# A routed mixture-of-experts kernel: the first slots' rows partly gathered during the output projection, routing steps reordered, expert numbers by rank read later

## The chip, the cores and the metric

The kernel runs on one core of one Trainium2 chip. The metric is the device time of one execution in microseconds; the time before is the median of three runs, 1043.46 us (1043.24 to 1044.73).

## What is computed

Two residual layers work on 512 tokens of width 1024. Layer 0 mixes the tokens with a gated unit, layer 1 with latent attention; both add a memory attention, and an output projection is added to `x`. Each layer ends with a routed mixture of 32 experts, 2 for each token:

```python
def hierarchical_moe(h, w_group, b_group, w_expert, b_expert, w_gate, w_up, w_down):
    ...
    g_idx = jnp.argmax(g_prob, axis=-1)              # one of 4 groups
    ...
    top_w, top_i = lax.top_k(e_prob, TOP_K)          # 2 of its 8 experts
    top_w = top_w / jnp.sum(top_w, axis=-1, keepdims=True)
    expert_id = g_idx[:, None] * EXPERTS_PER_GROUP + top_i
    weights = g_w * top_w
    combine = jnp.sum(jax.nn.one_hot(expert_id, N_EXPERTS, dtype=jnp.float32) * weights[..., None], axis=1)
    ...
        gate = jnp.einsum('td,edf->tef', xb, w_gate)
        up = jnp.einsum('td,edf->tef', xb, w_up)
        act = jax.nn.silu(gate) * up * cb[..., None].astype(xb.dtype)
        return jnp.einsum('tef,efd->td', act, w_down)
...
    x = x + jnp.concatenate([mix, mem_out], axis=-1) @ w_out
    x = x + hierarchical_moe(rms_norm(x, norm2_g[i]), ...)
```

All is float32. An expert has three weight matrices of 1 MiB, so a layer's experts are about 100 MB.

## The kernel before, in words

The 512 tokens are four row tiles of 128, held in SBUF as `K.x[t]`. TensorE, SP and GpSimd work in the order in which the code is written (`manual`, L1624); VectorE and ScalarE in an order that a scheduler chose. SBUF has 39 shared units for weights; a load into a unit waits until the unit's last reader is done. Stream loads leave from SP's queue.

**Output projection (`w_out`, L570).** Its last three chunks are done tile by tile: for each row tile two halves of three triples of products, then an addition into `K.x[t]` (L609). The function `rows` (L1633) returns steps for slots between the next tile's products: 0 and 1 turn the tile that is just finished for the router (`turn`, L807), 3 makes its logits (L821), 6 chooses its experts (`choose`, L830). `start` (L801) makes a tile's row scale (ScalarE squares, then GpSimd) and stores the tile to `h2d` in DRAM. The last tile has no next one; its steps and all placing are in `finish` (L1642).

**Routing.** `choose` works for batches of tiles ([0, 1], [2], [3]). VectorE finds the two experts and their one-hot marks `osum`; then the weights are made, by VectorE, ScalarE and six GpSimd steps (L883 to L891) that split them into bfloat16 parts in `K.vals`. `begin` (L967) places a batch: products of the marks with a triangle and with ones count the earlier tokens of the same expert (L901), VectorE turns the counts into slot numbers (64 slots for each expert), and builds `of` and `o`, which mark each token's slot. `carry(t)` (L981) multiplies `of` with the tile's rows, so that after four tiles the bank holds the rows of the first 128 slots (experts 0 and 1); it is copied to `x0`, one half by VectorE, the other by ScalarE. `fill` (L995) collects each slot's token number and weights, and `slots` (L1004) reads them.

**Order of experts.** Experts 0 to 5 are loaded before routing is known, during the projection (`ahead`, `rest`, L1659). The other 26 are ordered by how many tokens they have: `rank` (L911) compares their counts on VectorE, TensorE transposes the resulting list (L932), VectorE casts it to `ids` (L944), and SP reads it into registers (`expert`, L954), four or two numbers ahead of each step's loads.

**Expert steps (`moe`, L1036).** There are 14 steps of 128 slots: 3 with two experts by number, 2 with four by rank, 9 with two. A step gathers its rows from `h2d` by an indirect DMA from GpSimd's queue (`gather`, L1043, after a GpSimd memset to zero, since empty slots have an index out of bounds and are skipped), turns them, multiplies with gate and up (`gate_up`, 64 products for two experts), with down, and adds back. Only step 0 takes `x0`. `nxt(i)` lets SP load as many tiles as the steps so far have freed. Loads by number begin at `nxt(1)` in the code, and on SP they stand right behind the last tile's store:

```python
        R = routed(layer, phase, ahead, rest)
        R.g0 = R.slots(R.c0)
        ...
        R.rank()
...
    gather(1)
    xT = turn(0)
    gather(2)
    fills = R.group(1, 0)
    a = gate_up(0, xT)
    fills()
```

Of the kernel before, what the change touches and what calls it, by code (L numbers as in the profile page):

```python
# [13 lines left out]
I32 = mybir.dt.int32  # L14
# [771 lines left out]

class Route:
# [33 lines left out]
    def logits(self, t):  # L821
        K, nc = self.K, self.K.nc
        T = next(T for T in self.BATCHES if t in T)
        if t == T[0]:
            self.b = K.bank([2, 36])
        for k in range(8):
            K.last_mm = nc.tensor.matmul(self.b[:, t - T[0]], self.lg[t][:, k], K.wr[:, k],  # L827
                                         start=k == 0 and t == T[0], stop=k == 7, skip_group_check=True)

    def choose(self, t):  # L830
# [52 lines left out]
        tt(wr[:, :, 1, 0], wr[:, :, 0, 0], ex, ALU.mult, p)  # L883
        p.tensor_copy(wr[:, :, :, 1], bc(self.r[:, T].unsqueeze(2), [n, 2]))

        r1 = z_("r1", [2, 2])
        z = K.vals[:, T]
        p.tensor_copy(z[:, :, :, 2:4], wr)
        tt(r1, wr, z[:, :, :, 2:4], ALU.subtract, p)
        p.tensor_copy(z[:, :, :, 4:6], r1)  # L890
        tt(z[:, :, :, 6:8], r1, z[:, :, :, 4:6], ALU.subtract, p)  # L891
# [19 lines left out]
    def rank(self):  # L911
# [9 lines left out]
        e, w, move = z[:, 5, 0:1], z[:, 5, 2:4], z[:, 6, 0:2 * NT]  # L921
        less = K.k2([n, n], BF, "less")
# [8 lines left out]
        eb = K.bank([n], p=1)  # L931
        K.tr(eb, e[0:n])  # L932
# [10 lines left out]
        self.ids = K.s([n], I32, tag="k_ids", bufs=1, p=1)  # L943
        v.tensor_copy(self.ids, eb)  # L944
# [5 lines left out]
        v.tensor_max(K.over[self.i], w[:, 0:1], w[:, 1:2])  # L950

# [15 lines left out]
    def begin(self, batch):  # L967

        K, T = self.K, self.BATCHES[batch]
        self.place(T)  # L970
        for t in T:
            o, of = K.k1([128], F32, "o1"), K.k1([128], F32, "of")
            sl = self.slot[:, t]
            K.nc.vector.tensor_scalar(o, K.iota16[:, 0:128], sl[:, 0:1], None, op0=ALU.is_equal)
            K.nc.vector.scalar_tensor_tensor(out=of, in0=K.iota16[:, 0:128], scalar=sl[:, 1:2], in1=o, op0=ALU.is_equal,
                                             op1=ALU.add)
            self.of[t] = of
        for t in T:
            self.o[t] = self.mark(0, t)

    def carry(self, t):  # L981

        K = self.K
        if t == 0:
            self.c0 = K.bank([GROUPS[0][1], 8])
            self.b0 = [K.bank([512]) for _ in range(2)]
        for n in range(2):
            K.nc.tensor.matmul(self.b0[n], self.of[t], K.x[t][:, n * 512:n * 512 + 512], start=t == 0, stop=t == NT - 1)
        if t == NT - 1:
            self.x0 = K.k4([D], F32, "xg")  # L990
            K.nc.vector.tensor_copy(self.x0[:, 0:512], self.b0[0])
            K.nc.scalar.copy(self.x0[:, 512:1024], self.b0[1])
# [43 lines left out]
def moe(K, layer, R, X, nxt, on_rows, soon):  # L1036
# [6 lines left out]
    def gather(i):  # L1043
        g, c = place_of(i)
        xg[i] = K.k4([D], F32, "xg")
        K.gate(nc.gpsimd.memset(xg[i], 0.0), K.last_mm)  # L1046
# [84 lines left out]
    xT = turn(0)  # L1131
    gather(2)
    fills = R.group(1, 0)
    a = gate_up(0, xT)
    fills()
# [484 lines left out]
def build(tc, ctx, args, out):  # L1620
# [9 lines left out]
    def routed(layer, phase, ahead=None, rest=None, keep=False):  # L1630
        R = Route(K, layer, keep)

        def rows(t):  # L1633
# [3 lines left out]
            if t == NT - 1 and not keep:  # L1637
                return {0: [finish]}
            return {0: [lambda: R.turn(t, 0)], 1: [lambda: R.turn(t, 1)], 3: [lambda: R.logits(t)],
                    6: [lambda: R.choose(t)]}  # L1640

        def finish():  # L1642
            R.begin(0)
            for q in range(2):
                R.turn(NT - 1, q)
            R.logits(NT - 1)
            R.choose(NT - 1)
            R.carry(0)
            for batch, t in ((1, 1), (2, 2), (None, 3)):
                if batch:  # L1650
                    R.begin(batch)
                R.carry(t)
# [3 lines left out]
    def sparse(layer, phase, on_last, soon=lambda part: None):  # L1656
# [11 lines left out]
        R.rank()  # L1668
# [93 lines left out]
```

## Time and profile before

| | us |
|---|---|
| median of 3 runs | 1043.46 |
| lowest, highest run | 1043.24, 1044.73 |
| the profiled execution | 1043.92 |
| its span, first to last instruction | 1042.1 |
| TensorE busy in the span | 1004.9 |
| VectorE, ScalarE, GpSimd busy | 555.6, 432.6, 195.5 |

The times in the rows count from the start of the span. PE is TensorE, PEld its weight loads, DVE VectorE, ACT ScalarE, POOL GpSimd, SP the engine that issues most DMAs. An idle time in brackets stands before the instruction, with the instruction that ended it. The granted clock is a share of TensorE's full 2.4 GHz. One execution holds both layers, so each place of the change occurs twice: about 250 to 277 us, and about 787 to 813 us.

### The profile page before, as it was taken

How to read it: one execution, taken by the hardware profiler on the slowest of the kernel's cores; microseconds unless marked ns; L12 is line 12 of the kernel's file. 1: busy time of each engine (PE TensorE's matmuls, PEld its weight loads, DVE VectorE, ACT ScalarE, POOL GpSimd, SP SyncE). 2: the span in 40 equal slices, each digit the busy share in tenths (PEclk: the TensorE clock that was granted, in tenths of full speed). 3: DMA queues.
4: the chain of work that ended last, by engine and by line, in shares of the span. 5: the costliest groups of instructions: out<-in, count | busy, mean ns of one | idle time of the engine just before them, and what ended most of it. 6: DMA issues, size and time to landing. Idle time of an engine off the chain costs nothing. (4 is left out here: it accounts for less than half of the span.)

```text
span 1042.1 us, 18418 instructions
## 1 busy us (share of the span) xinstructions
PE 1004.9 (96%) x6438; PEld 743.8 (71%) x6438; DVE 555.6 (53%) x1343; ACT 432.6 (42%) x1172; POOL 195.5 (19%) x415
## 2 busy tenths in 40 slices
PE   8999999999899999999999999999998999999996
PEld 6878888887565666655878888878885666666653
DVE  5654685505464544434767777788027345445343
ACT  6845743414232313213747676778023223223130
POOL 2441110003110101100321553420014001011000
PEclk9999999999999999999999999999999999999998
DMA  9442424694699999999222111204964999999993
GB/s 354 134 139 50 150 71 145 237 409 179 239 408 407 407 407 405 408 407 395 87 54 82 51 28 42 75 18 132 368 278 165 387 408 407 407 407 408 407 404 128
DMA packets 82027, 262.94 MB, mean 252 GB/s; under 512 B 10172, under 2 KB 13472, under 8 KB 81925
## 3 DMA queue, kind: packets, MB, share of 16 engines
q1 hardware_dynamic: 75776, 247.10, 62.2%
q0 software_dynamic: 6144, 14.56, 4.2%
q8 instruction: 53, 0.87, 0.3%
q14 instruction: 50, 0.40, 0.1%
q10 hardware_dynamic: 4, 0.00, 0.0%
HBM read 260.08 MB, written 7.34 MB: 257 GB/s over the span
## 5 line engine op out<-in xcount | busy, mean ns | idle before, releaser
L1073 PE MATMUL ps<-xw,xT 128*64 128x256 f32 (+1 forms) x2048 | 209.6, 382 | 2.8 <-DMA xw<-in_moe_w_up_dram 2.4
L1073 PEld LDWEIGHTS ps<-xw,xT 128*64 128x64 f32 (+1 forms) x2048 | 131.1, 131 | 86.0 <-issue 17.4
L1119 DVE TENSOR_TENSOR x<-x,ps 128x512 f32<-128x512 f32 x216 | 133.4, 680 | 104.7 <-PE ps L1111 104.7
L1097 PE MATMUL ps<-xw,actT 128*64 128x512 f32 (+1 forms) x512 | 102.2, 597 | 0.0
L1110 PE MATMUL ps<-yh,cm 128*128 128x512 f32 x224 | 91.1, 407 | 0.0
L1078 ACT ACTIVATE silu<-ps,wsl 128x256 f32<-128x256 f32 x28 | 13.3, 474 | 183.9 <-PE ps L1073 183.9
L1111 PE MATMUL ps<-yl,cm 128*128 128x512 f32 x224 | 88.1, 393 | 0.1
L1046 POOL MEMSET xg<- 128x1024 f32 x26 | 24.8, 952 | 330.4 <-PE ps L128 278.1
L116 PE MATMUL ps<-wh,c 128*128 128x512 f32 x192 | 76.4, 398 | 0.0
L118 PE MATMUL ps<-wh,c 128*128 128x512 f32 x192 | 74.9, 390 | 0.0
L117 PE MATMUL ps<-wl,c 128*128 128x512 f32 x192 | 74.7, 389 | 0.0
L132 DVE TENSOR_TENSOR yl<-ps,yh 128x512 fp32r<-128x512 f32 x56 | 38.7, 691 | 59.9 <-ACT yh L131 59.9
L1097 PEld LDWEIGHTS ps<-xw,actT 128*64 128x64 f32 (+1 forms) x512 | 29.4, 130 | 52.8 <-issue 39.8
L1059 ACT ACTIVATE xT<-ps,G 128x128 f32<-128x128 f32 x224 | 60.8, 382 | 12.0 <-PE ps L128 11.8
L116 PE MATMUL ps<-wh,hh 128*128 128x512 f32 (+1 forms) x160 | 60.8, 380 | 2.2 <-ACT pm L453 1.1
L219 DVE SCALAR_TENSOR_TENSOR wl<-wr,G,wh 128x512 fp32r<-128x512 f32 (+1 forms) x80 | 55.1, 730 | 11.2 <-ACT wh L209 10.8
L117 PE MATMUL ps<-wl,hh 128*128 128x512 f32 (+1 forms) x160 | 59.8, 374 | 0.0
L118 PE MATMUL ps<-wh,hl 128*128 128x512 f32 (+1 forms) x160 | 59.7, 373 | 0.0
L144 ACT ACTIVATE junk<-x 128x512 bf16<-128x512 f32 x32 | 20.2, 631 | 90.0 <-DVE x L609 87.3
L609 DVE TENSOR_TENSOR x<-x,ps 128x512 f32<-128x512 f32 x16 | 11.0, 687 | 84.6 <-PE ps L118 84.6
L161 POOL TENSOR_SCALAR s1dt.float<-s2dt.float 128x1 f32<-128x1 f32 x18 | 6.9, 381 | 253.1 <-ACT junk L144 252.6
L1110 PEld LDWEIGHTS ps<-yh,cm 128*128 128x128 f32 x224 | 42.1, 188 | 17.0 <-issue 9.3
(369 smaller groups left out, 2046.0 us busy)
## 6 DMA issues: line engine op xcount, KB each, us to landing
xw<-in_moe_w_gate_dram SPq DMA_DIRECT2D x128, 512.0 KB, 10.1
xw<-in_moe_w_up_dram SPq DMA_DIRECT2D x128, 512.0 KB, 10.1
xw<-in_moe_w_down_dram SPq DMA_DIRECT2D x128, 512.0 KB, 10.8
wr<-in_a_w_in_dram SPq DMA_DIRECT2D x20, 512.0 KB, 4.7
wr<-in_a_w_out_dram SPq DMA_DIRECT2D x12, 512.0 KB, 3.4
wr<-in_b_w_out_dram SPq DMA_DIRECT2D x12, 512.0 KB, 3.6
wr<-in_w_mem_kv_dram SPq DMA_DIRECT2D x8, 512.0 KB, 9.9
wr<-in_b_w_in_dram SPq DMA_DIRECT2D x8, 512.0 KB, 10.6
```

The costliest lines, as they stand in the source:

```text
L116: mm(out, A[0], B[0], start=first, stop=False)
L117: mm(out, A[0], B[1], start=False, stop=False)
L118: self.last_mm = mm(out, A[1], B[0], start=False, stop=last)
L132: return self.nc.vector.tensor_sub(lo, src, hi.bitcast(F32))
L219: b = self.nc.vector.scalar_tensor_tensor(out=l, in0=r, scalar=g, in1=h.bitcast(F32), op0=ALU.mult, op1=ALU.subtract)
L1046: K.gate(nc.gpsimd.memset(xg[i], 0.0), K.last_mm)
L1059: nc.scalar.mul(xT[:, k], b[:, k % 4], K.gain(2 + layer, k))
L1073: nc.tensor.matmul(b[c, u], xT[:, k, c], X[i][h][k // 4 * 2 + u][:, k % 4], start=k == 0 and u == 0, stop=k == 7, skip_group_check=True, **tp)
L1097: nc.tensor.matmul(bs[n][c], aT[:, j, c], X[i][h][4 + j][:, n * 512:n * 512 + 512], start=j == 0, stop=j == 1, skip_group_check=True, **tp)
L1110: nc.tensor.matmul(b, cm[:, ts128(t)], yh[:, sl], start=first, stop=False)
L1111: K.last_mm = nc.tensor.matmul(b, cm[:, ts128(t)], yl[:, sl], start=False, stop=last)
L1119: v.tensor_add(K.x[t][:, sl], K.x[t][:, sl], b)
```

## The change

Six things change together. (1) Tiles 0 and 1 are placed (`begin(0)`) during tile 3's projection products, and `early` gathers their rows of the first 128 slots from `h2d` by an indirect DMA into `x0`, which ScalarE has zeroed; `of` and `carry` are left for tiles 2 and 3 alone, whose bank VectorE adds to `x0`. (2) The fills of tiles 0 and 1 follow in `early`. (3) Tile 2's placing stands in the middle of the last tile's logits, tile 3's right after the carry of tile 2. (4) The GpSimd weight steps of tiles 2 and 3 are made later (`R.weights()`), those of tile 2 behind the last tile's row scale. (5) `rank` stands behind `turn(0)`; the transpose of its list and the cast are a new function `numbers`, called after `gate_up(0)`. (6) The zeros of gathers 1 and 2 come from ScalarE.

```diff
+def zeros(K, tile):
+    K.nc.scalar.mul(tile, K.mhalf[:, 0:1].to_broadcast([128, tile.free_size()]), 0.0)
+    return tile
...
-    def logits(self, t):
+    def logits(self, t, mid=None):
...
         for k in range(8):
+            if k == 4 and mid is not None:
+                mid()
...
-    def choose(self, t):
+    def choose(self, t, defer=False):
...
-        tt(wr[:, :, 1, 0], wr[:, :, 0, 0], ex, ALU.mult, p)
-        p.tensor_copy(wr[:, :, :, 1], bc(self.r[:, T].unsqueeze(2), [n, 2]))
...
+        def weights():
+            tt(wr[:, :, 1, 0], wr[:, :, 0, 0], ex, ALU.mult, p)
+            p.tensor_copy(wr[:, :, :, 1], bc(self.r[:, T].unsqueeze(2), [n, 2]))
...
+        self.weights = weights
+        if not defer:
+            weights()
...
         v.scalar_tensor_tensor(out=je, in0=r, scalar=K.col, in1=mine, op0=ALU.is_equal, op1=ALU.mult,
                                accum_out=e)
-        eb = K.bank([n], p=1)
-        K.tr(eb, e[0:n])
...
-        self.ids = K.s([n], I32, tag="k_ids", bufs=1, p=1)
-        v.tensor_copy(self.ids, eb)
...
+    def numbers(self):
+
+        K = self.K
+        eb = K.bank([SORTED], p=1)
+        K.tr(eb, self.e_rank[0:SORTED])
+        self.ids = K.s([SORTED], I32, tag="k_ids", bufs=1, p=1)
+        K.nc.vector.tensor_copy(self.ids, eb)
...
         self.place(T)
-        for t in T:
+        for t in T if batch else ():
             o, of = K.k1([128], F32, "o1"), K.k1([128], F32, "of")
...
+    def early(self):
+
+        K, nc = self.K, self.K.nc
+        v = nc.vector
+        self.x0 = zeros(K, K.k4([D], F32, "xg"))
+        b = K.bank([8])
+        for t in self.BATCHES[0]:
+            for j in range(2):
+                nc.tensor.matmul(b, self.o[t][:, j, 0:128], K.vals[:, t, j], start=(t, j) == (0, 0),
+                                 stop=(t, j) == (1, 1))
+        tok, idx = K.s([1]), K.s([1], I32, tag="idx0", bufs=1)
+        v.tensor_reduce(tok, b[:, 0:2], axis=AX.X, op=ALU.add)
+        v.tensor_scalar(idx, tok, 1024.0, 0.0, op0=ALU.add, op1=ALU.max)
+        nc.gpsimd.indirect_dma_start(
+            out=self.x0, out_offset=None, in_=K.h2d[self.i][0:256],
+            in_offset=bass.IndirectOffsetOnAxis(ap=idx, axis=0), bounds_check=255, oob_is_err=False)
+        self.c0 = K.bank([GROUPS[0][1], 8])
+        for t in self.BATCHES[0]:
+            self.fill(self.c0, t, self.o[t])
+
     def carry(self, t):
...
-            self.x0 = K.k4([D], F32, "xg")
-            K.nc.vector.tensor_copy(self.x0[:, 0:512], self.b0[0])
-            K.nc.scalar.copy(self.x0[:, 512:1024], self.b0[1])
+            for n in range(2):
+                x0 = self.x0[:, n * 512:n * 512 + 512]
+                K.nc.vector.tensor_add(x0, x0, self.b0[n])
...
-        K.gate(nc.gpsimd.memset(xg[i], 0.0), K.last_mm)
+        if i < 3:
+            zeros(K, xg[i])
+        else:
+            K.gate(nc.gpsimd.memset(xg[i], 0.0), K.last_mm)
...
     xT = turn(0)
+    R.rank()
     gather(2)
     fills = R.group(1, 0)
     a = gate_up(0, xT)
+    R.numbers()
     fills()
...
             if t == NT - 1 and not keep:
+                R.weights()
                 return {0: [finish]}
...
+            todo = {0: [lambda: R.turn(t, 0)], 1: [lambda: R.turn(t, 1)], 3: [lambda: R.logits(t)],
+                    6: [lambda: R.choose(t, t == 2 and not keep)]}
+            if t == 2 and not keep:
+                todo[2] = [lambda: R.begin(0)]
+                todo[6].insert(0, R.early)
+            return todo
 
         def finish():
-            R.begin(0)
             for q in range(2):
                 R.turn(NT - 1, q)
-            R.logits(NT - 1)
-            R.choose(NT - 1)
-            R.carry(0)
-            for batch, t in ((1, 1), (2, 2), (None, 3)):
-                if batch:
-                    R.begin(batch)
-                R.carry(t)
+            R.logits(NT - 1, lambda: R.begin(1))
+            R.choose(NT - 1, True)
+            R.carry(2)
+            R.begin(2)
+            R.weights()
+            R.carry(3)
...
         nc.scalar.activation(K.s([1]), R.ex[:, 0:1], AF.Silu)
-        R.rank()
```

## Rows read from the trace of the kernel before

**Rows 1.** The page of the profile: the first line of its part 1, then one line of its part 2 (busy tenths of the DMA engines in 40 equal slices of the span), and one line of part 6 (the loads of gate tiles: count, KB each, median us from issue to landing).

```profile
PE 1004.9 (96%) x6438; PEld 743.8 (71%) x6438; DVE 555.6 (53%) x1343; ACT 432.6 (42%) x1172; POOL 195.5 (19%) x415
...
DMA  9442424694699999999222111204964999999993
...
xw<-in_moe_w_gate_dram SPq DMA_DIRECT2D x128, 512.0 KB, 10.1
```

**Rows 2.** Busy time of the engines in two stretches of the first expert stage. Columns: stretch and its length, busy us (instructions) of PE, PEld, DVE, ACT and POOL, granted TensorE clock, DMA share, GB/s.

```profile
275.00:300.00 25.00, 24.96 (x196) 15.02 (x194) 11.19 (x27) 8.37 (x24) 1.95 (x2) 1.00 1.03 408
...
450.00:475.00 25.00, 24.65 (x158) 16.00 (x156) 12.30 (x21) 6.75 (x21) 2.46 (x4) 1.00 1.02 406
```

**Rows 3.** DMA queues in 300 to 470 us: the line of the indirect gathers' queue (packets, MB, share of 16 engines).

```profile
q0 software_dynamic: 1584, 3.35, 5.2%
```

**Rows 4.** Timeline of the SP queue (start, us, line, operation, tile, count): the first and the last expert loads by number of layer 0, and the first of layer 1.

```profile
270.79 2.62 SPq L254 DMA_DIRECT2D xw<-in_moe_w_gate_dram  x4
...
471.95 4.19 SPq L254 DMA_DIRECT2D xw<-in_moe_w_down_dram  x4
...
807.07 2.68 SPq L254 DMA_DIRECT2D xw<-in_moe_w_gate_dram  x4
```

**Rows 5.** The chain of work that ended last, in the second expert stage (start, us, what): the first and the last of its three stretches of DMA, and what follows the last.

```profile
875.98 11.16 DMA xw<-in_moe_w_up_dram
...
989.41 11.27 DMA xw<-in_moe_w_up_dram
1000.73 3.24 PE ps L1073 x26
```

**Rows 6.** What SP waited for in 268 to 500 us (us in total, times, longest).

```profile
SPq L954 <- DVE rank L936: 16.5, 1, 16.5
SPq L254 <- PE ps L1073: 7.9, 15, 2.4
```

**Rows 7.** Timeline of VectorE in layer 0, from the last tile's choice of experts to the cast of the expert numbers.

```profile
256.17 0.26 DVE L843 SCALAR_TENSOR_TENSOR c_L<-ps,rr,br 128x36 f32<-128x36 f32 x1 [1.39 <-POOL rr L152]
...
259.16 0.30 DVE L963 TENSOR_SCALAR os<-iota,rs 128x384 bf16<-128x384 f16 x1
...
260.68 1.13 DVE L963 TENSOR_SCALAR os<-iota,rs 128x384 bf16<-128x384 f16 x1
...
263.29 0.69 DVE L991 COPY xg<-ps 128x512 f32<-128x512 f32 x1 [0.99 <-PE ps L988]
...
264.48 0.17 DVE L1013 TENSOR_SCALAR idx<-tok 128x3 int32<-128x3 f32 x1
...
267.83 0.17 DVE L944 CAST k_ids<-ps 1x26 int32<-1x26 f32 x1
```

**Rows 8.** The register loads of line 954 on SP over the whole run (ns min/median/max, first and last start in us).

```profile
L954 SPq TENSOR_LOAD <-k_ids x52: 261/267/468, 268.0 to 995.5; - x52
```

**Rows 9.** Timeline of TensorE in layer 0, from the last row tile's transposes to the second step's products (start, us, line, operation, tile, count, idle time before it and its releaser), and one line of layer 1.

```profile
250.53 1.60 PE L128 MATMUL ps<-ident,x 128*128 128x128 f32 x8
251.97 2.24 PE L827 MATMUL ps<-wr,hT 128*128 128x36 f32 x16
...
259.60 0.18 PE L901 MATMUL ps<-os,tri 128*128 128x32 bf16 x1 [1.35 <-DVE os L839]
...
262.12 1.98 PE L988 MATMUL ps<-x,of 128*128 128x512 f32 x4 [0.40 <-DVE of L975]
...
266.95 0.18 PE L128 MATMUL ps<-ident,rank 26*1 26x26 f32 x1 [2.60 <-DVE rank L929]
267.06 1.74 PE L128 MATMUL ps<-ident,xg 128*128 128x128 f32 x8
268.74 8.19 PE L1073 MATMUL ps<-xw,xT 128*64 128x256 f32 x64
...
278.52 5.40 PE L1073 MATMUL ps<-xw,xT 128*64 128x256 f32 x48
...
284.29 1.95 PE L1073 MATMUL ps<-xw,xT 128*64 128x256 f32 x16
...
805.52 7.75 PE L1073 MATMUL ps<-xw,xT 128*64 128x256 f32 x64
```

**Rows 10.** Timeline of GpSimd in layer 0, from the weights of tile 2 to the first gather.

```profile
253.29 0.38 POOL L839 TENSOR_TENSOR rw<-rw,c_ex 128x1 f32<-128x1 f32 x1 [1.36 <-DVE rw L882]
...
254.92 0.29 POOL L161 TENSOR_SCALAR s1dt.float<-s2dt.float 128x1 f32<-128x1 f32 x1
...
255.57 0.57 POOL L152 TENSOR_TENSOR rr<-s1dt.float,mhalf 128x1 f32<-128x1 f32 x1
...
260.76 0.95 POOL L1046 MEMSET xg<- 128x1024 f32 x1
265.50 1.18 POOL L1047 DMA_INDIRECT xg<-h2d,idx  x1 [3.79 <-DVE wsl L1015]
```

**Rows 11.** All indirect gathers of layer 0 in 225 to 500 us: time from issue to landing.

```profile
DMA to landing us min/median/max: 4.0/7.6/8.2
```

**Rows 12.** The columns of group 2 again, for three stretches around the first expert product of layer 0.

```profile
254.00:256.00 2.00, 2.00 (x13) 0.95 (x13) 0.78 (x4) 0.00 (x0) 1.61 (x7) 1.00 1.03 422
268.00:270.00 2.00, 2.00 (x10) 1.18 (x10) 1.97 (x12) 2.00 (x8) 0.96 (x1) 0.50 0.54 150
272.00:274.00 2.00, 2.00 (x22) 1.31 (x20) 0.00 (x0) 0.00 (x0) 0.00 (x0) 1.00 0.88 246
```

More of the change, by code (lines that the diff above doesn't have):

```diff
@@ L882, in choose @@
         v.reciprocal(wr[:, :, 0, 0], den)
-        tt(wr[:, :, 1, 0], wr[:, :, 0, 0], ex, ALU.mult, p)
-        p.tensor_copy(wr[:, :, :, 1], bc(self.r[:, T].unsqueeze(2), [n, 2]))
[L886 to L891, printed above, removed]
+        def weights():
+            tt(wr[:, :, 1, 0], wr[:, :, 0, 0], ex, ALU.mult, p)
+            p.tensor_copy(wr[:, :, :, 1], bc(self.r[:, T].unsqueeze(2), [n, 2]))
+            r1 = z_("r1", [2, 2])
+            z = K.vals[:, T]
+            p.tensor_copy(z[:, :, :, 2:4], wr)
+            tt(r1, wr, z[:, :, :, 2:4], ALU.subtract, p)
+            p.tensor_copy(z[:, :, :, 4:6], r1)
+            tt(z[:, :, :, 6:8], r1, z[:, :, :, 4:6], ALU.subtract, p)
+        self.weights = weights
+        if not defer:
+            weights()
     def place(self, T):
@@ L921, in rank @@
         e, w, move = z[:, 5, 0:1], z[:, 5, 2:4], z[:, 6, 0:2 * NT]
+        self.e_rank = e
         less = K.k2([n, n], BF, "less")
@@ L979, in begin @@
             self.o[t] = self.mark(0, t)
+    def early(self):
[16 more added lines that the diff above has]
+            self.fill(self.c0, t, self.o[t])
     def carry(self, t):
         K = self.K
-        if t == 0:
-            self.c0 = K.bank([GROUPS[0][1], 8])
+        if t == 2:
             self.b0 = [K.bank([512]) for _ in range(2)]
         for n in range(2):
-            K.nc.tensor.matmul(self.b0[n], self.of[t], K.x[t][:, n * 512:n * 512 + 512], start=t == 0, stop=t == NT - 1)
+            K.nc.tensor.matmul(self.b0[n], self.of[t], K.x[t][:, n * 512:n * 512 + 512], start=t == 2, stop=t == NT - 1)
         if t == NT - 1:
-            self.x0 = K.k4([D], F32, "xg")
-            K.nc.vector.tensor_copy(self.x0[:, 0:512], self.b0[0])
-            K.nc.scalar.copy(self.x0[:, 512:1024], self.b0[1])
+            for n in range(2):
+                x0 = self.x0[:, n * 512:n * 512 + 512]
+                K.nc.vector.tensor_add(x0, x0, self.b0[n])
         self.fill(self.c0, t, self.o[t])
@@ L1637, in rows @@
             if t == NT - 1 and not keep:
+                R.weights()
                 return {0: [finish]}
-            return {0: [lambda: R.turn(t, 0)], 1: [lambda: R.turn(t, 1)], 3: [lambda: R.logits(t)],
-                    6: [lambda: R.choose(t)]}
+            todo = {0: [lambda: R.turn(t, 0)], 1: [lambda: R.turn(t, 1)], 3: [lambda: R.logits(t)],
[4 more added lines that the diff above has]
+            return todo
         def finish():
-            R.begin(0)
             for q in range(2):
                 R.turn(NT - 1, q)
-            R.logits(NT - 1)
-            R.choose(NT - 1)
-            R.carry(0)
-            for batch, t in ((1, 1), (2, 2), (None, 3)):
-                if batch:
-                    R.begin(batch)
-                R.carry(t)
+            R.logits(NT - 1, lambda: R.begin(1))
[4 more added lines that the diff above has]
+            R.carry(3)
         phase(K, rows, ahead)
```

## The prediction

> **What bounds the kernel now.** I read the page first: TensorE is busy 96% of the span, but the DMA line shows two long runs of nines, one for each expert stage [rows 1]. The windows of the first stage decide between the two. TensorE is busy nearly all the time, and the DMA engines have a share of 1.02 to 1.03 at 406 to 408 GB/s from 275 us to 475 us [rows 2]. So the DMA has no free time there. The bytes agree: 26 experts are loaded by number, 6 tiles of 512 KB (0.524 MB) each [rows 1], 81.8 MB; eleven gathers of about 0.335 MB (3.35 MB for ten [rows 3]) add 3.7 MB; 85.5 MB at 407 GB/s are 210 us. The first of these loads leaves SP at 270.79, the last ends at 476.1 [rows 4] and lands about 10 us later [rows 1]: 215 us with start and landing. The chain says the same of layer 1: its pieces on the expert weights end at 887.1 and at 1000.7, and only TensorE's tail follows [rows 5]. The expert stage is thus a stream whose end is its start plus its bytes, and TensorE keeps its pace.
>
> What starts the stream? SP waited 16.5 us for one thing, the expert numbers by rank [rows 6]. The numbers' cast runs from 267.83 to 268.00 [rows 7], the register loads begin at 268.0 [rows 8], and the first load follows at 270.79, 2.8 us after the cast.
>
> **The change, first half: TensorE's start.** Before, the stretch from the last projection product to the first expert product at 268.74 is a chain through all engines. Times are of layer 0; layer 1 repeats it.
>
> Row scale of the last tile. The logits are done at 254.2 [rows 9], but VectorE's first step on them starts at 256.17, after 1.39 us for the row scale [rows 7]: GpSimd did six weight steps of tile 2 from 253.29, and the scale only from 254.92 to 256.14 [rows 10]. The change puts the weights behind the scale, but the early gather and two small subtractions ahead of it. The gather's index needs four small products and two VectorE steps after the last projection product: about 251.7 (an estimate). Before, a gather started 0.85 us after its index (264.65 to 265.50) and took 1.18 [rows 7, 10]. So the early one runs from 252.5 to 253.7, the subtractions to 254.2, the scale (1.22) to 255.4. Gain 0.7; bounds 0 and 2.0 (logits at once).
>
> Choice of the last tile, 256.17 to the placing product at 259.60: 3.43 us. VectorE's placing of tile 2 lies among these steps (one marking alone is 0.30 [rows 7]); it moves ahead, since its product now stands inside the logits. Gain 0.6; bounds 0 and 1.1. Placing to the carry product, 259.60 to 262.12: 2.52 us, with one marking at 1.13 instead of 0.30 while GpSimd's memset runs from 260.76 [rows 7, 10]. ScalarE now writes those zeros; gain 0.8; bounds 0 and 0.8.
>
> The removed carries of tiles 0 and 1, two times 1.98 us of TensorE, are worth nothing: they lay where it later waited 1.35 us at 259.60 [rows 9]. The marks and first fills go under the projection, whose products run on. The carry product (1.98) now starts at 260.0 instead of 262.12 and ends at 262.0; the second of the two additions (0.69, as the copy at 263.29) ends at 262.7. The gathered rows must be there at 261.1. Gathers took 4.0 to 8.2 us [rows 11], and the last prefetched expert is still loading then, DMA share 1.03 [rows 12]; issued at 252.5 they land by 256.5 to 260.7, just in time.
>
> Ranking leaves the path. TensorE waited 2.60 us for it ahead of the first gathered rows [rows 9]. The first half of these can now turn while the second is added; from the second addition I take 0.9 us to the first expert product (1.68 before from turn to product; bounds 0.65 and 1.7). So the product starts at 263.6 instead of 268.74: **5.1 us earlier**, in layer 1 at 800.4 instead of 805.52. The 4 small counting products of the ranking now precede it and fit while ScalarE scales the turned rows.
>
> **The change, second half: the stream's start.** The numbers are now transposed after all 64 products of the first step. Those took 8.1 us in layer 0 and 7.7 in layer 1 [rows 9]. Transpose and cast (0.18 and 0.17 [rows 9, 7]) with hand-overs are 0.5, then SP's 2.8. First load: 263.6 + 8.1 + 0.5 + 2.8 = 275.0 against 270.79, **4.2 us later**; layer 1: 800.4 + 7.7 + 0.5 + 2.8 = 811.4 against 807.07, 4.3 later. Something is regained: before, the ramp was slow (246 GB/s in 272 to 274 [rows 12]) because the fourth and later loads waited for tiles still being read; now eight tiles are free at once. I take 0.7 per layer, between 0 and 1.0. Delay of the stream: 3.5 + 3.6 = **7.1 us**. What waits behind SP's register load is every later load, and behind these the products of the fourth step on; TensorE's lead of 5.1 us ends in waits for weights. The ScalarE zeros (about 1 us each, an estimate from the memset's 0.95 [rows 10]) lie in its idle time; if they did not, the second and third gather would be late by that much, and these are needed a step later.
>
> One thing can shift this. The clock was 0.50 in 268 to 270 [rows 12], the lower level (1.2 GHz), after TensorE had waited; the first step took 8.19 us, the second step's two pieces only 5.40 + 1.95 = 7.35 [rows 9]. I keep the slow figure since the waits that precede it remain. The Trainium skill ("TensorE: Matmul & The Clock Gate", "What's actually happening") calls the throttled clock the default, released by activity; by that the removed carries make the start colder, not warmer, and the trace's 0.50 after a wait agrees. At the full clock the delay would be 0.4 to 0.8 us less per layer.
>
> **Sum.** The profiled execution took 1043.92 us, its span 1042.1. 1043.92 + 7.1 = 1051.0; the median of the three runs is 0.46 lower, so 1050.6. All good bounds at once (product 7.2 us earlier, full clock, ramp 1.0) still delay the stream by 0.4 and 0.9: 1044.8. All bad ones (gather late, gains lost, product only 2.2 earlier, the cast 1 us behind another VectorE step, no ramp gain) give 8.1 + 8.2: 1059.8. Half way on either side is 1047.7 to 1055.2.
>
> **Rivals.** *TensorE is the bound.* Then its lead stays: 1043.5 - 2 x 5.1 = 1033.3. For it: 96% busy, and SP waited 7.9 us on products [rows 6], so tiles, not bytes, may hold the stream. Against: the share of 1.03 while it did so. It decides if DMA share falls below 1 in mid stage. The Trainium skill ("Perfetto Trace Analysis", "Identifying the Most-Contended Engine") holds matmul busy time for no measure of closeness to the bound; no run so far shows that here by itself. Chance 0.12.
>
> *The later stream catches up.* An earlier TensorE frees tiles sooner, so SP's 7.9 us of waits on products vanish; if half of each layer's were bytes lost, that repays 3.5 us per layer: 1043.5. Against it again the saturated share. Chance 0.07.
>
> *The early rows do not come early.* If the gather lands after about 263.5 (behind the last expert's tiles, or behind the store of tile 2), the first product starts hardly earlier and the numbers still come after it: about 1060. Chance 0.05.
>
> The forecast has 0.76. A change under 0.2% (2.1 us) is no change for this measurement. Faster is the first rival, 0.12; same the second, 0.07; slower the rest, 0.81. The range 1043.5 to 1055.5 holds nearly all of the forecast and the second rival.
>
> **What the changed profile would show.** The first expert product near 263.6 and 800.4; the numbers' transpose behind its 64 products; the first load by number near 275.0 and 811.4; the hole in DMA before it longer; the share in the stage still 1.03; TensorE's waits for expert weights up by about 8.6 us per layer (5.1 + 3.5), in the fourth to sixth step; the chain passing through these loads. The forecast is wrong if the first load leaves no later than before, or if it does and the stage ends no later.

## The result, and the profile after

The changed kernel takes 1055.76 us, the median of five runs (1053.49 to 1058.18), against 1044.57 (1043.24 to 1044.86) for the kernel before on the same chip: a ratio of 1.0112, with a 95% interval of 1.0098 to 1.0125. It is slower, as forecast, but by 11.2 us and not by 7.1, and 0.3 us outside the range. The profiled execution of the changed kernel took 1053.49 us, span 1051.8; it is the fastest of the five, so the trace below explains 9.6 us against the traced execution of before, and what the slower ones add is read from the run a_again.

The page after, with its lines for TensorE and for the DMA engines (40 slices), against [rows 1]:

```profile
PE 1007.6 (96%) x6430; PEld 741.8 (71%) x6430; DVE 555.4 (53%) x1341; ACT 437.3 (42%) x1176; POOL 194.5 (18%) x413
...
DMA  9432423794699999999222111213954999999993
```

TensorE's 96% is unchanged although the kernel is 9.7 us longer in span. The share of a whole run again says nothing. The Trainium skill ("Perfetto Trace Analysis", "Identifying the Most-Contended Engine") calls matmul busy time no good measure of how close a kernel is to the roofline, and here the trace agrees: 96% before, 96% after.

The windows after, columns as in [rows 2]: two early stretches that answer to [rows 12], the two of [rows 2], and one in between.

```profile
254.00:256.00 2.00, 0.77 (x1) 0.50 (x2) 1.90 (x14) 0.00 (x0) 0.52 (x3) 0.75 1.02 408
256.00:258.00 2.00, 2.00 (x4) 0.73 (x3) 0.83 (x6) 0.20 (x1) 0.94 (x5) 0.50 0.72 283
...
275.00:300.00 25.00, 25.00 (x189) 14.67 (x185) 9.90 (x23) 5.74 (x15) 1.96 (x2) 1.00 1.00 382
325.00:350.00 25.00, 20.24 (x204) 10.34 (x196) 9.20 (x21) 4.59 (x13) 1.96 (x2) 1.00 1.03 406
450.00:475.00 25.00, 23.77 (x157) 14.88 (x154) 8.87 (x16) 4.67 (x13) 2.47 (x4) 1.00 1.03 408
```

Two things are to be seen. Once the stream runs, the DMA engines are as full as before (1.03, 406 to 408 GB/s), and now TensorE has holes: 4.8 us of 25 in 325 to 350, where it was busy for all 25.00 before. And ahead of the expert stage the granted clock falls to 0.50, the 1.2 GHz level, in 256 to 258, after a stretch in which TensorE was busy 0.77 of 2 us; before, it was busy for all of 254 to 256 [rows 12].

The SP queue after (the loads of [rows 4]: first of layer 0, last of layer 0, first of layer 1), then SP's wait for the numbers and its longest wait on products in 268 to 500 us, against [rows 6]:

```profile
274.34 2.23 SPq L254 DMA_DIRECT2D xw<-in_moe_w_gate_dram  x4
...
476.00 4.20 SPq L254 DMA_DIRECT2D xw<-in_moe_w_down_dram  x4
...
816.67 2.24 SPq L254 DMA_DIRECT2D xw<-in_moe_w_gate_dram  x4
```

```profile
SPq L972 <- DVE k_ids L968: 21.3, 1, 21.3
SPq L254 <- PE ps L1113: 5.1, 17, 0.4
```

The first load by number is 3.55 us later than before, the last 4.05, the first of layer 1 9.60. SP's wait for the numbers is 21.3 us where it was 16.5.

TensorE after, against [rows 9]:

```profile
255.23 3.55 PE L1025 MATMUL ps<-x,of 128*128 128x512 f32 x4 [1.89 <-DVE of L993]
...
258.84 0.18 PE L914 MATMUL ps<-os,tri 128*128 128x32 bf16 x1
260.56 1.98 PE L1025 MATMUL ps<-x,of 128*128 128x512 f32 x4 [1.54 <-DVE of L993]
...
262.54 1.54 PE L128 MATMUL ps<-ident,xg 128*128 128x128 f32 x8
...
264.10 7.13 PE L1113 MATMUL ps<-xw,xT 128*64 128x256 f32 x64
271.16 0.18 PE L128 MATMUL ps<-ident,rank 26*1 26x26 f32 x1
...
806.70 7.13 PE L1113 MATMUL ps<-xw,xT 128*64 128x256 f32 x64
```

The last projection product starts at 248.58 in this execution and at 250.21 in that of before, a difference between executions and not of the change: in a_again, the same changed kernel, it starts at 250.32. So I measure each layer from its own last projection product, P (layer 1: 790.77 after, 786.75 before).

| us after P, layer 0 / layer 1 | before | after |
|---|---|---|
| first expert product | 18.53 / 18.77 | 15.52 / 15.93 |
| first load by number | 20.58 / 20.32 | 25.76 / 25.90 |
| end of the last load's issue | 225.93 / 225.54 | 231.62 / 231.18 |
| last row less the row above it | 205.35 / 205.22 | 205.86 / 205.28 |

This closes the sum. The stream starts 5.18 us later in layer 0 and 5.58 in layer 1, and takes 0.51 and 0.06 longer: 11.33. Less the 1.63 us by which this execution reached P earlier, that is 9.70, the difference of the spans. TensorE's head start of 3.0 and 2.8 us appears nowhere in it.

The chain that ended last, in layer 1, against [rows 5]: it still passes through the expert weights, the last such piece ends at 1010.3, and TensorE's tail follows.

```profile
885.59 10.78 DMA xw<-in_moe_w_up_dram
...
999.55 10.78 DMA xw<-in_moe_w_up_dram
1010.38 3.24 PE ps L1113 x26
```

### The profile page after: what moved, and what is told of

Its sections match the earlier page's. It is cut to its first block, busy times and chain, and to the rows that moved or that the text cites. A ratio compares the mean times of both kernels' runs of the same rounds, so it can differ in the third digit from the quotient of the medians.

```text
span 1051.8 us, 18406 instructions
## 1 busy us (share of the span) xinstructions
PE 1007.6 (96%) x6430; PEld 741.8 (71%) x6430; DVE 555.4 (53%) x1341; ACT 437.3 (42%) x1176; POOL 194.5 (18%) x413
## 3 DMA queue, kind: packets, MB, share of 16 engines
q0 software_dynamic: 6432, 14.83, 4.2%
## 5 line engine op out<-in xcount | busy, mean ns | idle before, releaser
L1113 PE MATMUL ps<-xw,xT 128*64 128x256 f32 (+1 forms) x2048 | 215.3, 383 | 12.4 <-DMA xw<-in_moe_w_up_dram 11.5
L1086 POOL MEMSET xg<- 128x1024 f32 x22 | 20.9, 952 | 340.7 <-PE ps L128 297.0
```

The lines of the kernel that those rows point to most:

```text
L1113: nc.tensor.matmul(b[c, u], xT[:, k, c], X[i][h][k // 4 * 2 + u][:, k % 4], start=k == 0 and u == 0, stop=k == 7, skip_group_check=True, **tp)
```

## The experiments

Each starts from the changed kernel or from the kernel before, as its edit says. First the table of what they measured, all offsets from P (layer 0 / layer 1), since every verdict below rests on it.

| run | us, median (range) | ratio to before, 95% | first product | first load by number | load to last load |
|---|---|---|---|---|---|
| a_mid | 1050.89 (1049.38–1052.34) | 1.0061 [1.0044, 1.0078] | 17.56 / 15.41 | 25.62 / 23.21 | 205.1 / 204.9 |
| b_late | 1052.82 (1051.21–1053.86) | 1.0078 [1.0061, 1.0095] | 15.28 / 15.28 | 25.52 / 25.25 | 205.1 / 205.6 |
| b_static | 1041.45 (1037.37–1044.38) | 0.9972 [0.9958, 0.9987] | 18.80 / 18.79 | 1.58 / 1.56 | |
| a_static | 1035.26 (1034.29–1037.16) | 0.9919 [0.9902, 0.9935] | 17.55 / 15.28 | 1.80 / 1.78 | |
| a_warm | 1052.63 (1051.74–1054.49) | 1.0100 [1.0080, 1.0121] | 15.43 / 15.24 | 25.67 / 25.22 | 205.4 / 205.5 |
| a_warm_choice | 1053.73 (1051.68–1055.15) | 1.0098 [1.0076, 1.0121] | 15.37 / 15.09 | 25.61 / 25.07 | 205.0 / 205.6 |
| a_rank_warm | 1041.98 (1039.11–1043.87) | 0.9986 [0.9974, 0.9997] | 19.02 / 16.48 | 20.89 / 18.08 | 206.3 / 206.5 |
| b_rank | 1041.01 (1039.72–1043.63) | 0.9984 [0.9973, 0.9995] | 16.28 / 16.28 | 18.15 / 17.89 | 205.6 / 207.2 |
| a_again | 1056.07 (1054.40–1057.42) | 1.0111 [1.0092, 1.0130] | 17.55 / 17.04 | 27.79 / 27.01 | 205.3 / 205.0 |
| a_choice2 | 1051.44 (1051.10–1052.63) | 1.0072 [1.0051, 1.0093] | 14.51 / 14.23 | 24.75 / 24.20 | 204.8 / 205.7 |
| a_best | 1045.04 (1041.89–1048.05) | 1.0013 [1.0000, 1.0027] | 15.05 / 14.78 | 20.55 / 20.00 | 205.7 / 206.2 |
| b_best | 1045.94 (1044.35–1047.23) | 1.0011 [1.0001, 1.0021] | 15.27 / 15.27 | 21.89 / 21.57 | 205.2 / 205.0 |

The kernel before took 1044.45 beside the first four, 1043.37 beside the next four and 1043.78 beside the last four.

The last column is the theory in one place. With the numbers known only at run time, first products from 14.2 to 19.0 us after P and first loads from 17.9 to 27.8 gave streams of 204.8 to 207.2 us. The streams of 206.2 us and more all have a first load at 20.9 us or sooner, so a part of an early start is given back.

**a_mid: the numbers half a step earlier.**

```diff
-    a = gate_up(0, xT)
-    R.numbers()
+    a = gate_up(0, xT, {4: R.numbers})
```

> The kernel after, with the numbers' transpose and cast in the middle of the first step's products (ahead of the 5th of 8 chunks) instead of behind them. Theory A (the stream of expert loads starts 2.8 us after the numbers' cast, and the stage ends with the stream): the cast comes 3.5 us earlier in each layer (half of 7.1 us of products), the first load by number near 270.9 us on the changed kernel's time scale, the run 6.9 us shorter: about 1048.9. Theory B (the 11 us come from TensorE's waits and its lower clock after them, or from work that the change added, not from the stream's start): no change, about 1055.8.

Measured 1050.89. In layer 1 the first load came 2.7 us earlier after P than in the changed kernel's trace (half of the first step's products take 3.6), and the last load 3.1 us earlier (228.10 against 231.18). In layer 0 it came hardly earlier, because in this execution both carries ran at the low clock and the first product was 2 us late. The sign is the theory's; its size has two further causes. One is the carries, which the next pairs take apart. The other is the cast: the transpose ran at 270.52 in layer 0 and at 810.67 in layer 1, the cast only at 272.03 and 812.18, 1.5 us later, since VectorE still had markings ahead of it. In the changed kernel it is 0.2 us later (271.16 to 271.37). That is 1.3 of the 3.6 us.

**b_late: of the whole change, the late numbers alone.** The kernel before, with only the transpose and the cast of the numbers taken out of the ranking and put behind the first step's products.

```diff
-        eb = K.bank([n], p=1)
-        K.tr(eb, e[0:n])
...
+    def numbers(self):
...
     a = gate_up(0, xT)
+    R.numbers()
```

> The kernel before, with one part of the change alone: the numbers' transpose and cast behind the first step's products. Theory A: TensorE does not wait 2.6 us for the ranking, so the first product starts near 266.4 instead of 268.74, its 64 products end near 274.5, the first load follows near 277.8 instead of 270.79; 7.0 us later in each layer: about 1058.6. Theory B: the first product is 2.3 us earlier and nothing else is worse: 1040 to 1044.

Measured 1052.82, 8.4 us over before, so this part alone makes most of the loss. TensorE in layer 0 of it:

```profile
262.78 1.33 PE L128 MATMUL ps<-ident,xg 128*128 128x128 f32 x8
264.05 7.13 PE L1078 MATMUL ps<-xw,xT 128*64 128x256 f32 x64
271.10 0.18 PE L128 MATMUL ps<-ident,rank 26*1 26x26 f32 x1
```

The first product came 15.28 us after P in both layers, 3.3 to 3.5 us earlier than before and as early as the changed kernel's, with no early gather, no deferred weights and all four carries still there. So what TensorE gains in the changed kernel is the ranking's 2.60 us off its path [rows 9], and the rest of the first half brought it nothing in sum; its parts, below, cancel. I had expected this kernel slower, since I gave the product a smaller lead and its products 8.1 us; they took 7.1.

**b_static and a_static: no numbers to wait for.** The kernel before and the changed kernel with the experts taken in a fixed order, so the weights used are not those that the routing asks for. The work and the bytes are the same.

```diff
-                ids = [R.expert(rank + h) for h in range(WIDTH[i])]
+                ids = [FIXED + rank + h for h in range(WIDTH[i])]
```

> The kernel before, but the loads by number take experts 6 to 31 in fixed order, so SP waits for no numbers; the sorting has then no effect on which weights are used. Same bytes, same products. Theory A: the stream is now started by free tiles: three spare tiles load early, the rest as the first step frees them, an effective start some 2.5 to 3 us earlier per layer: 1038 to 1040, unless TensorE's own pace takes over (then 1040 to 1042). Theory B: SP's wait was not what counted: 1044.6.

> The kernel after with the same fixed order of experts, so that the place of the numbers does not count. Theory A: all of the 11 us go, and the first product, about 3 us earlier per layer than before, frees tiles that much earlier: 4 to 6 us below the kernel before with fixed order, 1033 to 1036. Theory B: still 8 to 11 us above the kernel before with fixed order.

Measured 1041.45 and 1035.26. Waiting for the numbers cost the kernel before 3.0 us and the changed kernel 20.5 (against its 1055.76). Two readings follow. In the kernel before, the free tiles held the stream nearly as late as the numbers did: without the numbers its last load ends 0.7 and 1.4 us earlier after P (225.22 and 224.18 against 225.93 and 225.54), and no more. And with the numbers out of the way, an earlier first product does free tiles earlier: a_static takes 6.2 us less than b_static. One window shows where, first of b_static and then of a_static, columns as before:

```profile
260.00:285.00 25.00, 21.95 (x171) 13.69 (x171) 10.26 (x37) 5.43 (x19) 4.11 (x5) 0.86 0.58 211
```

```profile
260.00:285.00 25.00, 24.84 (x193) 14.67 (x193) 10.47 (x39) 7.18 (x21) 2.17 (x2) 0.92 0.70 261
```

The stream fills earlier, 261 against 211 GB/s around the first product (262 where the window is moved by the 1.55 us by which a_static reaches P sooner). In both runs three loads leave for tiles that are free, the early ones of the table; the fourth waits for a tile that the first step frees, and leaves 24.22 and 22.67 us after P in b_static, 20.82 and 18.55 in a_static. So the early start would have been worth 6 us, had the stream not been tied to the numbers.

**a_again: the changed kernel once more.** Nothing edited.

> The changed kernel once more, unaltered, beside the next three. Theory C (TensorE idles before the carry of tile 2 and its clock falls): that carry takes 3.5 to 3.8 us instead of 1.98 in both layers; the carry of tile 3 takes 1.98 or 3.8 as it falls, and with 3.8 the first product comes 17.5 instead of 15.5 us after the last projection product. Median 1053.5 to 1056, runs spread over 4 us.

Measured 1056.07, the same as the first five runs' 1055.76 within their spread; the profiled execution took 1056.98. Its carries in layer 0, and one window:

```profile
256.95 3.78 PE L1025 MATMUL ps<-x,of 128*128 128x512 f32 x4 [1.88 <-DVE of L993]
...
262.54 3.78 PE L1025 MATMUL ps<-x,of 128*128 128x512 f32 x4 [1.54 <-DVE of L993]
```

```profile
262.00:264.00 2.00, 1.46 (x2) 0.84 (x3) 0.71 (x3) 0.00 (x0) 0.00 (x0) 0.50 0.00 0
```

Here the second carry too ran at clock 0.50 and took 3.78 us instead of 1.98, so the first product came 17.55 us after P instead of 15.52 and the first load 27.79 instead of 25.76: 2.0 us, which is the difference of the carries plus 0.2. Of the changed kernel's five first runs the slowest (1058.18) has the lowest mean clock, 0.981, and the fastest 0.991. The lead of the change thus varies from execution to execution with the clock, and the median of 1055.76 lies between this execution and the one first traced.

**a_warm: TensorE kept busy.** The changed kernel with four products of no use, three ahead of tile 2's carry and one ahead of tile 3's.

```diff
+        def warm(n):
+            b = K.bank([512])
+            for _ in range(n):
+                nc.tensor.matmul(b, K.ident, K.x[0][:, 0:512], start=True, stop=True)
...
+            warm(3)
             R.carry(2)
             R.begin(2)
+            warm(1)
```

> The kernel after, with four spare products (ident times a row tile, read by nobody) put where TensorE waits: three ahead of the carry of tile 2, one ahead of the carry of tile 3. Theory A with C (the removed carries had kept TensorE at the full clock; without them it idles, falls to 0.50, and the carries of tiles 2 and 3 take up to 3.8 us instead of 1.98, differently from run to run): both carries take 1.98 in both layers, the first product comes 15.3 to 15.5 us after the last projection product in both layers, the first load by number 25.3 to 25.6 after it, runs within 2 us of each other, median 1053 to 1054. Rival (the spread of the runs has another cause): 1055.8 and a spread of 4 to 5 us as before.

The carries of layer 0:

```profile
255.59 1.88 PE L1025 MATMUL ps<-x,of 128*128 128x512 f32 x4
...
260.24 1.98 PE L1025 MATMUL ps<-x,of 128*128 128x512 f32 x4 [0.58 <-DVE of L993]
```

Both carries are at 1.9 to 2.0 us in both layers, and the first product is at 15.43 and 15.24. Over all traces with the carries of tiles 0 and 1 gone: without spare products (the changed kernel, a_again, a_mid, a_static) tile 2's carry is slow, at 3.5 us or more, in all eight stages; with them (a_warm, a_warm_choice, a_choice2, a_best, a_rank_warm) both carries are at 1.9 to 2.0 in nine of ten. So the slow carries are those at the low clock, and products in TensorE's wait mostly prevent it. That this makes the kernel faster is not shown: 1052.63 is 3 us under the changed kernel's median, but the intervals of the two ratios overlap.

**a_warm_choice and a_choice2: the last tile's choice.** In the changed kernel VectorE waited for one subtraction of GpSimd. Here it does that subtraction itself, and tile 3 is placed ahead of tile 2's carry; three spare products stand ahead of the placing. a_warm_choice has the fourth one too, ahead of tile 3's carry; a_choice2, whose edit this is, leaves it out.

```diff
-        tt(g, Lg, bc(gm.unsqueeze(2), [n, 4]), ALU.subtract, p)
+        tt(g, Lg, bc(gm.unsqueeze(2), [n, 4]), ALU.subtract)
...
+            warm(3)
+            R.begin(2)
             R.carry(2)
-            R.begin(2)
```

> The same, and two more steps: the subtraction ahead of the group softmax runs on VectorE instead of GpSimd (where it stands behind the six weight steps of tile 2), and tile 3 is placed before the carry of tile 2. If the lost part of TensorE's lead is that wait and that order: placing of tile 3 1.1 to 1.5 us earlier, first product 14.0 to 14.5 us after the last projection product, first load 24.2 to 24.7 after it, about 2 us less than with the spare products alone: 1051 to 1052. Otherwise no change against it.

> The kernel after with three spare products ahead of tile 3's placing, that placing ahead of tile 2's carry, and the subtraction before the group softmax on VectorE. Nothing stands ahead of the carry of tile 3 but tile 2's. If VectorE's 1.08 us wait for that softmax is what ate the rest of TensorE's lead: first product 14.3 to 14.6 us after the last projection product, first load 24.5 to 24.8 after it, 0.7 to 1 us less per layer than with spare products alone (1052.6): about 1051. If not, 15.3 and 25.5 again.

a_warm_choice missed its expectation. The placing product moved from 10.19 to 9.02 us after P, but tile 2's carry and the spare product now stood between it and tile 3's carry on TensorE's queue, and the first product stayed at 15.37. Without the spare one (a_choice2) it came at 14.51 and 14.23, about 1 us earlier, the first load at 24.75 and 24.20, and the time was 1051.44. VectorE's wait is gone in it, and the last tile's choice takes 3.75 us (255.59 to 259.34 in layer 0) where it takes 4.94 in the changed kernel. The gain of about 1 us per layer is that of the three steps together, the subtraction, the order and the spare product left out; their shares in it are not separated.

**b_rank and a_rank_warm: the numbers early.** The ranking ahead of the last carry, and its transpose and cast at once behind that carry, in the kernel before (b_rank) and in a_warm (a_rank_warm).

```diff
+                    R.rank()
                 R.carry(t)
...
+            R.numbers()
...
-        R.rank()
```

> The kernel before with the early ranking alone: counting products and ranking ahead of the carry of tile 3, the numbers' transpose right behind it. Theory A: numbers' cast near 15.5, first load near 18.5, first product near 17 us after the last projection product: 1040 to 1042, about as good as the changed kernel with the same ranking, so the early gather and the reordering bring nothing that the ranking's place does not. Rival (they do bring TensorE a lead): 2 us or more slower than that kernel.

> The kernel after with the spare products, and the ranking started as soon as tile 3's experts are known (ahead of its carry), the numbers' transpose behind that carry and ahead of the first turn. Theory A: the numbers are cast some 16 us after the last projection product, the first load leaves about 19 us after it (before 20.4, after 25.8); TensorE's first product waits for the transpose and comes at about 17. The stream is then held by free tiles, about 2 us per layer earlier than before: 1040 to 1041, faster than both kernels. Theory B: no better than after with spare products.

TensorE in layer 0 of b_rank:

```profile
264.44 0.18 PE L128 MATMUL ps<-ident,rank 26*1 26x26 f32 x1 [0.94 <-DVE rank L933]
264.55 1.23 PE L128 MATMUL ps<-ident,xg 128*128 128x128 f32 x8
265.75 0.44 PE L1078 MATMUL ps<-xw,xT 128*64 128x256 f32 x2
```

The wait for the ranking shrank from 2.60 us to 0.94, and both the product and the load came 2.2 to 2.5 us earlier than before. The kernel took 1041.01, a ratio of 0.9984 [0.9973, 0.9995]: faster than both kernels, but only by 2.4 us (1.7 by the ratio) where the load moved 2.4 us in each of two layers. In layer 0 the last load ended 2.2 us earlier (223.71 after P). In layer 1 only 0.4, its stream being the longest of all, 207.2 us, and its ramp is where that lies:

```profile
800.00:825.00 25.00, 24.96 (x215) 16.43 (x215) 10.76 (x40) 9.37 (x30) 3.25 (x3) 1.00 0.88 330
```

The window begins 2.80 us ahead of the first load. The same stretch of before (804.27 to 829.27) had 352 GB/s; 22 GB/s less for 25 us are 0.55 MB, or 1.4 us of stream. In layer 0 it is 340 against 350 GB/s. Longer waits for free tiles do not show in this ramp: from the first load on, SP waited 2.6 us in 25 for TensorE's work, against 7.3 before, and 9.7 for earlier loads, against 6.6. What slowed the ramp, and why it cost layer 1 more than layer 0, is open.

a_rank_warm came to 1041.98, the same as b_rank. It is 13.8 us under the changed kernel and 10.7 under a_warm, from which it differs only in the place of the ranking and of the numbers. That is the cleanest verdict: this place makes the loss. With the ranking early, the early gather and the reordering bring nothing more.

**a_best and b_best: early ranking, transpose behind the first products.**

```diff
-    a = gate_up(0, xT)
-    R.numbers()
+    a = gate_up(0, xT, {1: R.numbers})
...
+            R.rank()
             R.carry(3)
```

> As the run with the subtraction on VectorE, and with the ranking begun ahead of tile 3's carry and the numbers' transpose behind the first of the 8 chunks of the first step's products, so that neither waits for the other. Theory A: first product 15.0 to 15.5, first load 19.0 to 19.8 us after the last projection product; the stream is then held by free tiles alone, as with experts in fixed order (1035.3): 1036 to 1039, below both kernels. Theory B: no better than 1042.

> The kernel before with the early ranking and the numbers' transpose behind the first chunk of the first step's products, nothing else of the change. Theory A: first product 15.3 to 15.8, first load 19.2 to 20 us after the last projection product: 1037 to 1040, within 2 us of the kernel with all other parts of the change. If the early gather and the reordering do count, 2 us or more slower than that.

Both missed: 1045.04 and 1045.94. In layer 1 of a_best TensorE turned the numbers at 801.90; VectorE's part shows why it didn't help:

```profile
802.40 1.09 DVE L981 TENSOR_SCALAR os<-iota,rs 128x512 bf16<-128x512 f16 x3
803.41 0.17 DVE L968 CAST k_ids<-ps 1x26 int32<-1x26 f32 x1
```

The cast ran 1.5 us after the transpose, behind four slot markings that had been scheduled ahead of it. In layer 0 of b_best it was 2.7 us (265.68 to 268.33). The product's lead over b_rank, 1.0 to 1.5 us, bought nothing; the load's delay of 2.1 to 3.7 us per layer cost 3 us in the whole by the ratios to before (4 to 5 by the medians). This is the change's own exchange, on a smaller scale. Against the kernel before, a_best shows it with the loads held still: they leave at 20.55 and 20.00 us after P, before at 20.58 and 20.32, the first products come 3.5 and 4.0 us earlier, and the time is the same (1.0013 [1.0000, 1.0027]).

## Why the prediction was right about the mechanism and wrong about the size

**The bound.** Right. The stream by number lasts 205 to 207 us from its first load, with first products from 14.2 to 19.0, and the time follows the first load. *TensorE is the bound* is refuted by b_late and a_rank_warm, whose first products are as early as or later than the changed kernel's while the times follow the loads, and by a_best, whose early products gain nothing. *The later stream catches up* is refuted by the table: 205.86 and 205.28 us after, 205.35 and 205.22 before. SP's wait on the gate and up products did shrink, from 7.9 [rows 6] to 5.1 us, and nothing came back for it.

**The numbers' delay.** Right in each piece. The transpose stands behind the 64 products (271.16), the cast follows at 271.37, the first load at 274.34, 2.80 us after the cast's end; 2.8 were predicted. The products took 7.1 us at the full clock, not 8.1 and 7.7.

**TensorE's waits.** Right in sum, half right in kind. From the first expert product of layer 0 (264.10) to the first product behind the stage (503.62) it is 239.5 us, and 231.0 before: 8.5 more, about the 8.6 predicted. But these were to be waits for weights, and only half of them are. The waits for expert weights, by TensorE, in 264 to 480 us after:

```profile
PE ps L1113 <- DMA xw<-in_moe_w_up_dram: 5.3, 8, 1.3
PE ps L1113 <- DMA xw<-in_moe_w_gate_dram: 0.8, 1, 0.8
```

and in 268 to 480 before:

```profile
PE ps L1073 <- DMA xw<-in_moe_w_up_dram: 1.7, 4, 0.5
```

That is 6.1 us against 1.7, 4.4 more, between 329 and 350 in the fifth and sixth step. The rest shows as longer busy time: from the first product on TensorE was busy 229.6 us until 500, and 225.5 until 496 before, and in 340 to 365, behind the waits, the granted clock was 0.93.

**TensorE's head start: the step that failed.** 5.1 us were predicted, 3.0 and 2.8 came. VectorE and GpSimd in layer 0 after, against [rows 7] and [rows 10]:

```profile
253.90 0.26 DVE L851 SCALAR_TENSOR_TENSOR c_L<-ps,rr,br 128x36 f32<-128x36 f32 x1 [0.99 <-POOL rr L152]
...
254.53 0.31 DVE L981 TENSOR_SCALAR os<-iota,rs 128x384 bf16<-128x384 f16 x1
...
257.21 0.16 DVE L883 TENSOR_REDUCE c_sg<-c_eg 128x1 f32<-128x4 f32 x1 [1.09 <-ACT c_eg L882]
...
261.73 0.69 DVE L1029 TENSOR_TENSOR xg<-xg,ps 128x512 f32<-128x512 f32 x1 [0.99 <-PE ps L1025]
```

```profile
251.14 1.11 POOL L1012 DMA_INDIRECT xg<-h2d,idx  x1 [3.36 <-PE ps L128]
...
255.39 0.20 POOL L847 TENSOR_TENSOR rw<-rw,c_ex 128x1 f32<-128x1 f32 x1 [1.52 <-DVE rw L890]
...
256.59 0.20 POOL L847 TENSOR_TENSOR vals<-c_r,vals 128x4 bf16<-128x4 f32 x1
256.74 0.20 POOL L847 TENSOR_TENSOR c_g<-c_L,c_gm 128x4 f32<-128x4 f32 x1
```

- *Row scale*: 0.7 predicted. The step on the logits starts 5.32 us after P and 5.96 before: 0.64, right.
- *Early gather*: it left at 251.14 and landed 7.7 us later at 258.8, and its rows were needed at 261.73. In time, as the forecast had it; the rival that made it late is refuted.
- *Placing to carry*: 258.84 to 260.56, 1.72 us; 1.7 predicted.
- *Second addition to first product*: it ends at 263.27, the product starts at 264.10, 0.83; 0.9 predicted.
- *Choice of the last tile*: wrong. "It moves ahead, since its product now stands inside the logits", with a gain of 0.6: 2.8 us. Measured 4.94 (253.90 to 258.84), 1.5 longer than before. Tile 2's markings still lay among VectorE's steps (254.53), because its counting product had been done only at 252.4. And VectorE stood 1.09 us before the sum of exponents (257.21): it needs a subtraction of GpSimd (256.74), and that, though its input was there at 254.35, waited behind tile 2's six weight steps (255.39 to 256.79), which the change had moved to just there. I had counted those steps as gone from in front of the row scale and not asked what they were now in front of. In a_choice2, which has this subtraction on VectorE, the choice takes 3.75 us, so the wait is worth about 1.2. The 2.1 us by which choice missed (a gain of 0.6 forecast, a loss of 1.5 measured) are the whole shortfall of the head start in layer 0.
- *"The removed carries of tiles 0 and 1 … are worth nothing"*: wrong in part. They lay in time in which TensorE waited later, but while they ran the clock was at 1.00 (254 to 256 in [rows 12]). Without them TensorE waits 1.89 us and the granted clock is 0.50. The carry of tile 2 takes 3.55 us and not 1.98, and in other executions that of tile 3 as well (a_again). In b_late, which keeps the four, each takes 1.96 to 1.98. The removed carries need not be the whole reason: in layer 1 after, the clock had fallen to 0.58 already in 794 to 796, during the logits, ahead of the place where they stood. The Trainium skill ("TensorE: Matmul & The Clock Gate", "What's actually happening") makes the throttled clock the default, released by activity; these rows agree. The prediction drew from it that the start gets colder, and then gave that no price.

**The ramp.** Wrong: 0.7 us per layer were to come back because eight tiles are free at once. None did: first to last load took 0.51 and 0.06 us longer. The ramp itself is no faster: in the 25 us from the first load on the DMA engines moved 371 GB/s in both layers, before 377 and 381. The forecast took waits for tiles as what made the ramp before slow (246 GB/s [rows 12]); what does is open.

**The sum.** From the prediction's own place for the first load (275.0 and 811.4 less P of before: 24.8 and 24.65), the late product (2.1 and 2.3) less the faster products (1.0 and 0.6) and hand-overs (0.2 and 0.5) gives +1.0 and +1.25; the missing ramp gain adds 0.7 twice: 3.65. With 7.1 that is 10.75, the 5.18 + 5.58 measured; the longer streams add 0.57. The sign, the mechanism and the place were right; the size failed in the choice step, in the ramp and, for the median, in the carries' clock. The range missed the median by 0.3 us, because its upper end went half way to the bad case, and three terms (choice, ramp, clock of the carries) went bad together. That it missed by no more is in part luck: the first step's products, kept at the slow figure, ran 1.6 us faster over both layers and hid as much of the miss.

## What to carry to other kernels

When a stage is a saturated stream, find what starts it and follow that one thing through a change: work gained on any other engine ends as a wait for the stream, and each microsecond by which its first load is later counted here nearly in full (11.3 us of delay in the stage ends for 10.8 in the first loads). An earlier first load need not: in b_rank 4.9 us over both layers gave about 2. When steps are deferred, ask not only what they leave the front of, but what they now stand in front of on the same queue. Before dropping products that fill a wait on TensorE, look at the granted clock around them: the next ones on the path may run at half speed.

## What the runs showed of the hardware that was not expected

- The same four carry products took 1.88 to 1.98 us at a granted clock of 1.00 and 3.48 to 3.78 at 0.50, and the same kernel met one or the other in different executions and layers; its times spread over 4.7 us (1053.49 to 1058.18), those of the kernels with spare products over 1.5 (a_choice2) to 3.5 (a_warm_choice).
- Spare products are no sure cure: in layer 0 of a_rank_warm they ran slowly themselves, the first three taking 5.47 us where they took 2.82 in a_warm, and the first expert product came at 19.02. The clock had fallen to 0.66 already in 252 to 254, in which TensorE was busy for all of 2.00 us (as in layer 1 after, 794 to 796), and in the kernel before it stayed at 1.00 in 258 to 260, in which it was busy for 0.65; so the wait just ahead is not all that decides.
- The stream of expert loads by number kept 404 to 409 GB/s in stretches of 25 us and a length within 2.4 us in eleven kernels whose first loads differed by 9.9 us.
- The early gathers landed 7.7 and 6.7 us after their issue, while the last prefetched expert was still loading. They move about 0.13 MB each (an estimate: their queue moved 14.83 MB after and 14.56 before, with two gathers more), and yet took as long as the gathers of about 0.335 MB during the stream, with a median of 7.6 [rows 11].
